# Sums of weight blocks and combinations of h on VectorE in place of POOL, in a two-layer trunk on one core

## Chip, cores and metric

One core of a Trainium2 chip (trn2). The metric is device time in microseconds (us) of one execution of the whole program, the median of the runs. TensorE (PE) multiplies matrices; its weights are loaded by a sequencer that the profile calls PEld. VectorE (DVE), ScalarE (ACT) and GpSimd (POOL) work element by element, SyncE (SP) issues the large transfers. SBUF is the memory on the chip, PSUM the eight banks that TensorE writes to.

## What is computed

Two layers of a hybrid trunk over 512 prompt tokens and 8 sample tokens, all in float32. Each layer is a half-step SwiGLU FFN, a mixing layer (DeltaNet heads beside attention heads), and a second half-step FFN. The change lies in the four FFNs:

```python
def _modulate(x, g, shift, scale):
    return _rms_norm(x, g) * (1.0 + scale) + shift

def _swiglu(h, w_gu, w_down):
    a, b = jnp.split(h @ w_gu, 2, axis=-1)
    return (jax.nn.silu(a) * b) @ w_down

def _layer(x, c, pos, conv_buf, S0, k_buf, v_buf, prm):
...
    m = _adaln(c, w_ada, b_ada)
    h = _modulate(x, g_ffn1, m[:, 0], m[:, 1])
    x = x + 0.5 * m[:, 2] * _swiglu(h, w_ffn1_gu, w_ffn1_down)
...
    h = _modulate(x, g_ffn2, m[:, 6], m[:, 7])
    x = x + 0.5 * m[:, 8] * _swiglu(h, w_ffn2_gu, w_ffn2_down)
    return x, conv_new, S_new, k_new, v_new
```

The model has 1024 features (eight blocks of 128) and 2816 hidden features in each FFN (22 blocks of 128, called f).

## The kernel before

**Layout.** Features lie on the 128 partitions, tokens along the row: 520 columns, in two halves of 256 and 264 (`HALF`, line 23). A float32 product is made of three products in a rounded format: each weight block of 128 x 512 is split into `whi`, a rounded copy that ScalarE makes, and `wlo`, the rest, which VectorE gets as block minus `whi` (`Stream.rest`, line 266); h is split likewise into `hh` and `hl`. TensorE then adds `whi` x `hh`, `whi` x `hl` and `wlo` x `hh`.

**The stream of weights.** `Stream` (line 166) brings weights in: SyncE's queue moves blocks of 128 x 1024 into four raw buffers (two pairs), `advance` (225) issues the transfer of the next block when a raw buffer is free, splits the blocks and puts them into a ring of eight `whi` and `wlo`; `take` (280) hands them to TensorE in order.

**Seven products in place of eight.** For all but the first few f of an FFN, up and gate are computed together by a scheme of Winograd's: `seven` (line 880) makes seven products of 12 matmuls each out of a pair of raw blocks. Its weights are three raw quarters (a11, a12, a22) and four sums of quarters. `add_pair` (189) lists the sums, s1 = a21 + a22, s2 = s1 - a11, s3 = a11 - a21, s4 = a12 - s2; `add_up` (205) issues them when the pair has been sent for. Three f in each FFN (four in the first) are done in the plain way, so there are 75 sevens, and 300 sums. In a seven the products P1 to P7 go to PSUM banks `pb`, `pa`, `pb`, `pc`, `pb`, `pc`, `pb` in turn; `pa` and `pc` are the two banks of one tile that the trace calls `acc`, `pb` is called `aux`. Copies and additions between them (`u1`, `u2`) and the SwiGLU product (`t0`, `t1`: the trace's `g`) follow each product: `g<-acc,u` of 256 columns adds P1 to P2, `g<-acc,u` of 264 adds to P6, `g<-g,aux` multiplies by P7, `g<-g,u` of 264 multiplies the second half, and `ghi`, `glo` split the result for the down projection.

**Combinations of h.** The seven products need three combinations of the blocks of h, made once for each FFN by `combine` (line 798): for each of four k, `y0` and `y1` (each 128 x 2 x 264) out of `ht`, the modulated h before its shift is added, and the shift `sh`; ScalarE and VectorE split these into `th`. The head of an FFN is the stretch in which the norm of x, h, its combinations and the plain f are made, between the last down projection or mixing layer and the first seven.

**Order.** Each engine works through its own queue in order. The code runs once when the program is built; a model of the engines' time (`Clock`, line 40) tells `Stream` how far to run ahead and `Fill` (93) when to put in pieces of side work such as `combine`, which is written as a generator: each `yield` says what must be there before it goes on. All ScalarE work here is issued by `act` (336; its line in the trace is 344), all VectorE work by `_dve` (351; line 352), POOL's by `pool` (361; line 365), matmuls by `mm` (315; line 317), transfers by `dma` (310; line 311).

Of the kernel before, what the change touches and what calls it, by code (L numbers as in the profile page):

```python
# [9 lines left out]
F32 = mybir.dt.float32  # L10
# [155 lines left out]
class Stream:  # L166
# [38 lines left out]
    def add_up(self, j, must):  # L205

        clk = self.ops.clk
        while self.sums and self.sums[0][0] <= j + 2 and self.sums[0][5] < self.nd:
            n, q, x, y, op, d1 = self.sums[0]
            if n > must and clk.ready([self.raw[d1]]) > clk.pe + 1.0:  # L210
                return
            self.sums.pop(0)
            t = self.made[q] = self.new_sum()
            self.ops.pool("tensor_tensor", out=t, in0=self.source(x), in1=self.source(y), op=op)
            self.used(x)
            self.used(y)

# [74 lines left out]
class Ops:  # L292
# [43 lines left out]
    def act(self, **k):  # L336
        func = k["func"]
        if func in TABLE:
            self.table(TABLE[func])
        src = k["in_"]  # L340
        cost = (0.05 if self.psum(src) else 0.093) + 0.000835 * self.cols(src)
        cost += 0.093 * (hasattr(k.get("bias"), "tensor") or hasattr(k.get("scale"), "tensor"))
        cost += 0.093 * ("accum_out" in k)
        self.nc.scalar.activation(**k)  # L344
        self.clk.run("act", cost, self.aps(k, ("out", "accum_out")), self.aps(k, ("in_", "bias", "scale")))
# [15 lines left out]
    def pool(self, f, **k):  # L361
        if f == "memset":
            self.nc.gpsimd.memset(k["out"], k["value"])
        else:
            getattr(self.nc.gpsimd, f)(**k)  # L365
        self.clk.run("pool", 0.1 + 0.003 * self.cols(k["out"]), [k["out"]], self.aps(k, ("in_", "in0", "in1")))

    def tt(self, **k):
        self._dve("tensor_tensor", self.cols(k["out"]), k)

    def stt(self, **k):
        self._dve("scalar_tensor_tensor", self.cols(k["out"]), k)
# [22 lines left out]
def trunk(ctx, tc, xT, cT, cst, rope, vec, gu1, dn1, win, wba, wout, gu2, dn2, ada,  # L395
# [17 lines left out]
    def slot(name, dt=F32, shape=(128, NT), own=False):  # L413
        t = slot_p.tile(list(shape), dt, tag="s", name=name, bufs=SLOTS)
        if not own:
            used.add(t.tensor.name)
        return t

    def drop(*tiles):
        for t in tiles:  # L420
            used.remove(t.tensor.name)
# [376 lines left out]
    def combine(norm, th):  # L798

        ht = norm.ht
        sh = mt[norm.l][:, 3 * norm.j * 8:3 * norm.j * 8 + 8, 0]
        ys = []
        for k in range(4):
            yield lambda: norm.made[1] >= k + 5
            y0, y1 = (slot("y", F32, (128, 2, 264)) for _ in range(2))
            d = slot("d", F32, (128, 264))
            h1, h2 = ht[k], ht[k + 4]
            pool("tensor_tensor", out=y0[:, 0], in0=h1[:, 1], in1=h1[:, 0], op=ALU.subtract)  # L810
            pool("tensor_tensor", out=d, in0=h2[:, 1], in1=h2[:, 0], op=ALU.subtract)
            pool("tensor_tensor", out=y1[:, 1], in0=y0[:, 0], in1=d, op=ALU.subtract)
            drop(d)
            ys.append((y0, y1))
        yield lambda: norm.done[1] >= KD
        ds = small("dsh", (128, 4))
        tt(out=ds, in0=sh[:, 4:8], in1=sh[:, 0:4], op=ALU.subtract)
        xs = []

        def rest(k):  # L820
            (y0, y1), x = ys[k], xs[k]
            tt(out=x[1], in0=y0, in1=x[0].bitcast(F32), op=ALU.subtract)
            tt(out=x[3], in0=y1, in1=x[2].bitcast(F32), op=ALU.subtract)
            drop(y0, y1)
            th.append(x)

        for k in range(4):
            y0, y1 = ys[k]
            yield y0,
            h1, h2 = ht[k], ht[k + 4]  # L830
            stt(out=y0[:, 1], in0=h2[:, 1], scalar=sh[:, k + 4:k + 5], in1=y0[:, 0], op0=ALU.add, op1=ALU.subtract)
            stt(out=y1[:, 0], in0=h2[:, 1], scalar=ds[:, k:k + 1], in1=h1[:, 1], op0=ALU.add, op1=ALU.subtract)
            drop(h1, h2)
            if k:
                rest(k - 1)
            x = [slot("th", F32R, (128, 2, 264)) for _ in range(4)]
            act(out=x[0], in_=y0, func=AF.Copy)
            act(out=x[2], in_=y1, func=AF.Copy)
            xs.append(x)
        yield y1,  # L840
        rest(3)

    def ffn(l, j, norm, nxt, last, first=None, plain=3):
# [36 lines left out]
        def seven():  # L880

            pa, pb, pc = banks.pop(0) if banks else (None, aux(), None)
            if pa is None:
                u = acc()
                pa, pc = u[:, 0], u[:, 1]
            if pb is None:
                pb, pc = aux(), aux()
            t = slot("g")  # L890
            u1, u2 = (slot("u", F32, (128, 2, 264)) for _ in range(2))
            t0, t1 = t[:, 0:256], t[:, 256:520]

            def of_h(a, k0, n):
                return lambda _, part, k: hh[a][part][:, k0 + k, 0:n]

            def of_t(i, c, n=264):
                return lambda _, part, k: th[k][i + part][:, c, 0:n]

            def prod(bank, n, src, first):  # L900
                w = W.take()
                for k in range(4):
                    mmk(bank[:, 0:n], w, k, src, k, 0, first and k == 0, k == 3, join=not first)
                    W.advance(W.out - 1)
                    fill.step()
                go()

            prod(pb, 264, of_h(0, 0, 264), True)
            act(out=u1[:, 0], in_=pb[:, 0:264], func=AF.Copy)
            prod(pa, 256, of_h(0, 4, 256), True)  # L910
            tt(out=t0, in0=pa[:, 0:256], in1=u1[:, 0, 0:256], op=ALU.add)
            prod(pb, 264, of_t(0, 1), False)
            act(out=u1[:, 1], in_=pb[:, 0:264], func=AF.Copy)
            act(out=t0, in_=t0, func=AF.Silu)
            prod(pc, 264, of_t(0, 0), True)
            act(out=u2[:, 1], in_=pc[:, 0:264], func=AF.Copy)
            prod(pb, 264, of_t(2, 0), False)
            act(out=u2[:, 0], in_=pb[:, 0:264], func=AF.Copy)
            prod(pc, 264, of_h(1, 4, 264), False)
            tt(out=t1, in0=pc[:, 0:264], in1=u1[:, 1], op=ALU.add)  # L920
            tt(out=u2[:, 1], in0=u2[:, 1], in1=u2[:, 0], op=ALU.add)
            prod(pb, 256, of_t(2, 1, 256), False)
            act(out=t1, in_=t1, func=AF.Silu)
            tt(out=t0, in0=t0, in1=pb[:, 0:256], op=ALU.mult)

            def end():
                tt(out=t1, in0=t1, in1=u2[:, 1], op=ALU.mult)
                drop(u1, u2)

            later(end, *split(t))  # L930
# [1123 lines left out]
```

## Time and profile before

| | |
|---|---|
| median of 3 runs | 2265.32 us (2263.36 to 2268.89) |
| the profiled execution | 2262.45 us |
| its span, first to last instruction | 2260.2 us |
| mean granted clock of TensorE | 0.980 of full speed |
| TensorE busy (PE), 17254 matmuls | 2146.8 us, 95% |
| weight loads (PEld) | 2018.0 us, 89% |
| VectorE busy | 1590.3 us, 70% |
| ScalarE busy | 1109.7 us, 49% |
| POOL busy | 575.1 us, 25% |

Busy time says how full an engine is, not what sets the end. For that one goes to TensorE's waits, each of which names the engine and the tile that ended it, and from there to the timelines of the other engines at that place: what stood in the queue ahead of the instruction that TensorE waited for, and how long that took. An instruction's duration in a timeline runs from its start to its end; the next one on the same engine can start a little before that end, so the pace of an engine is read from starts.

### The profile page before, as it was taken

Reading aid. Unit: us, or ns where it says so; the run is one execution under the profiler, and the core shown is the slowest. Engines: PE = TensorE matmul, PEld = TensorE weight load, DVE = VectorE, ACT = ScalarE, POOL = GpSimd, SP = SyncE. Lnnn points to the kernel's source line nnn. Section 1 sums busy time; section 2 is a strip of 40 time slices with the busy share of each in tenths; the row PEclk is TensorE's granted clock in tenths of the full one; section 3 lists DMA queues with packets and bytes.
Section 4 is the critical chain, followed back from the end, with each engine's and each line's share of the span. In section 5 each row is a group of like instructions: output and inputs, shape, how many; then the busy total and the mean of one; then the engine's idle time right before and its main releaser. Section 6 shows DMA issues by size and latency. Waiting matters only on the chain. (4 is left out here: it accounts for less than half of the span.)

```text
span 2260.2 us, 44335 instructions
## 1 busy us (share of the span) xinstructions
PE 2146.8 (95%) x17254; PEld 2018.0 (89%) x17254; DVE 1590.3 (70%) x3246; ACT 1109.7 (49%) x2417; POOL 575.1 (25%) x487
## 2 busy tenths in 40 slices
PE   6899999998988999999998999999989889999999
PEld 4798899997877879889998999999888878999999
DVE  5783596567777778448749947955687778865972
ACT  4462365356645446336535634644646445653651
POOL 0440352001021135025305505500010203523530
PEclk9999999999999999999999999999999999999999
DMA  8538634343233564773332332334332242332332
GB/s 283 182 125 306 228 98 140 108 92 97 71 88 91 195 217 152 268 249 113 104 95 66 100 108 89 107 94 107 92 84 79 68 141 72 104 105 92 104 106 72
DMA packets 177538, 287.79 MB, mean 127 GB/s; under 512 B 50448, under 2 KB 96176, under 8 KB 177328
## 3 DMA queue, kind: packets, MB, share of 16 engines
q1 hardware_dynamic: 177328, 284.96, 40.2%
q8 instruction: 135, 2.21, 0.4%
q14 instruction: 75, 0.61, 0.1%
HBM read 271.55 MB, written 14.41 MB: 127 GB/s over the span
## 5 line engine op out<-in xcount | busy, mean ns | idle before, releaser
L344 ACT ACTIVATE whi<-raw 128x512 fp32r<-128x512 f32 (+1 forms) x597 | 361.3, 616 | 397.4 <-PE acc L317 313.2
L352 DVE TENSOR_TENSOR wlo<-raw,whi 128x512 fp32r<-128x512 f32 (+1 forms) x597 | 436.2, 749 | 62.3 <-ACT whi L344 61.3
L317 PE MATMUL acc<-hh,whi 128*128 128x256 f32 (+1 forms) x1640 | 430.9, 299 | 32.3 <-ACT g L344 12.8
L317 PE MATMUL acc<-hh,wlo 128*128 128x256 f32 (+1 forms) x1640 | 409.1, 286 | 12.1 <-DVE wlo L352 12.1
L317 PE MATMUL acc<-hl,whi 128*128 128x256 f32 (+1 forms) x1640 | 408.6, 286 | 1.7 <-DVE hl L352 1.5
L365 POOL TENSOR_TENSOR sum<-raw 128x512 f32<-128x512 f32 x150 | 214.0, 1427 | 662.4 <-DMA raw<-in_gu 384.7
L317 PEld LDWEIGHTS acc<-hh,whi 128*128 128x128 f32 x1640 | 290.8, 192 | 68.8 <-issue 35.8
L352 DVE TENSOR_TENSOR wlo<-sum,whi 128x512 fp32r<-128x512 f32 x300 | 319.4, 1083 | 36.2 <-ACT whi L344 35.2
L317 PE MATMUL aux<-th,whi 128*128 128x264 f32 (+1 forms) x1800 | 335.0, 283 | 1.0 <-ACT u L344 0.9
L317 PEld LDWEIGHTS acc<-hh,wlo 128*128 128x128 f32 x1640 | 289.9, 192 | 14.7 <-DVE wlo L352 14.6
L317 PEld LDWEIGHTS acc<-hl,whi 128*128 128x128 f32 x1640 | 289.6, 192 | 2.6 <-DVE hl L352 2.5
L317 PEld LDWEIGHTS aux<-th,whi 128*128 128x128 f32 x1800 | 277.0, 188 | 4.8 <-issue 3.4
L317 PE MATMUL acc<-ghi,whi 128*128 128x256 f32 (+1 forms) x1320 | 273.9, 283 | 2.7 <-DVE x L352 2.7
L317 PE MATMUL acc<-glo,whi 128*128 128x256 f32 (+1 forms) x1320 | 272.1, 282 | 0.0
L317 PE MATMUL acc<-ghi,wlo 128*128 128x256 f32 (+1 forms) x1320 | 271.6, 282 | 0.0
L317 PE MATMUL aux<-th,wlo 128*128 128x264 f32 (+1 forms) x900 | 254.4, 283 | 0.0
L352 DVE SCALAR_TENSOR_TENSOR x<-acc,mt,x 128x256 f32<-128x256 f32 x136 | 61.6, 480 | 236.0 <-PE acc L317 236.0
L317 PEld LDWEIGHTS acc<-ghi,whi 128*128 128x128 f32 x1320 | 206.4, 188 | 16.8 <-issue 16.8
L344 ACT ACTIVATE whi<-sum 128x512 fp32r<-128x512 f32 x300 | 186.2, 622 | 50.1 <-PE acc L317 45.4
L317 PEld LDWEIGHTS acc<-ghi,wlo 128*128 128x128 f32 x1320 | 207.1, 188 | 0.0
L317 PEld LDWEIGHTS acc<-glo,whi 128*128 128x128 f32 x1320 | 206.8, 188 | 0.0
L317 PE MATMUL aux<-hl,whi 128*128 128x264 f32 x604 | 172.0, 285 | 1.8 <-DVE hl L352 1.7
(325 smaller groups left out, 3979.1 us busy)
## 6 DMA issues: line engine op xcount, KB each, us to landing
raw<-in_gu SPq DMA_DIRECT2D x176, 512.0 KB, 3.6
ada<-in_ada SPq DMA_DIRECT2D x288, 256.0 KB, 5.6
raw<-in_dn SPq DMA_DIRECT2D x64, 512.0 KB, 3.6
raw<-in_win SPq DMA_DIRECT2D x44, 512.0 KB, 3.8
raw<-in_dn SPq DMA_DIRECT2D x64, 192.0 KB, 3.2
raw<-in_wout SPq DMA_DIRECT2D x22, 512.0 KB, 4.5
s<-in_s SPq DMA_DIRECT2D x16, 256.0 KB, 3.8
bv<-vnd SPq DMA_DIRECT2D x16, 256.0 KB, 4.1
```

The lines of the kernel that those rows point to most:

```text
L317: self.nc.tensor.matmul(out, lhsT=lhsT, rhs=rhs, start=start, stop=stop, skip_group_check=join)
L344: self.nc.scalar.activation(**k)
L352: getattr(self.nc.vector, f)(**k)
L365: getattr(self.nc.gpsimd, f)(**k)
```

## The change

Three things are changed. The sums in `add_up` are issued to VectorE. In `combine` the three POOL instructions for each k go; all four parts of `y0` and `y1` are made on VectorE in the loop that follows, three of them with the shift in the same instruction, and there is no tile `d`. In `seven` ScalarE's copy of P5 into `u2[:, 0]` goes; VectorE adds P5 to `u2[:, 1]` from its bank, at once behind P5 and not behind P6.

```diff
--- before.py
+++ after.py
@@ -211,7 +211,7 @@
                 return
             self.sums.pop(0)
             t = self.made[q] = self.new_sum()
-            self.ops.pool("tensor_tensor", out=t, in0=self.source(x), in1=self.source(y), op=op)
+            self.ops.tt(out=t, in0=self.source(x), in1=self.source(y), op=op)
             self.used(x)
             self.used(y)
 
@@ -802,16 +802,6 @@
         ht = norm.ht
         sh = mt[norm.l][:, 3 * norm.j * 8:3 * norm.j * 8 + 8, 0]
         ys = []
-        for k in range(4):
-            yield lambda: norm.made[1] >= k + 5
-            y0, y1 = (slot("y", F32, (128, 2, 264)) for _ in range(2))
-            d = slot("d", F32, (128, 264))
-            h1, h2 = ht[k], ht[k + 4]
-            pool("tensor_tensor", out=y0[:, 0], in0=h1[:, 1], in1=h1[:, 0], op=ALU.subtract)
-            pool("tensor_tensor", out=d, in0=h2[:, 1], in1=h2[:, 0], op=ALU.subtract)
-            pool("tensor_tensor", out=y1[:, 1], in0=y0[:, 0], in1=d, op=ALU.subtract)
-            drop(d)
-            ys.append((y0, y1))
         yield lambda: norm.done[1] >= KD
         ds = small("dsh", (128, 4))
         tt(out=ds, in0=sh[:, 4:8], in1=sh[:, 0:4], op=ALU.subtract)
@@ -825,11 +815,13 @@
             th.append(x)
 
         for k in range(4):
-            y0, y1 = ys[k]
-            yield y0,
+            y0, y1 = (slot("y", F32, (128, 2, 264)) for _ in range(2))
+            ys.append((y0, y1))
             h1, h2 = ht[k], ht[k + 4]
+            tt(out=y0[:, 0], in0=h1[:, 1], in1=h1[:, 0], op=ALU.subtract)
             stt(out=y0[:, 1], in0=h2[:, 1], scalar=sh[:, k + 4:k + 5], in1=y0[:, 0], op0=ALU.add, op1=ALU.subtract)
             stt(out=y1[:, 0], in0=h2[:, 1], scalar=ds[:, k:k + 1], in1=h1[:, 1], op0=ALU.add, op1=ALU.subtract)
+            stt(out=y1[:, 1], in0=h2[:, 0], scalar=sh[:, k + 4:k + 5], in1=y0[:, 1], op0=ALU.add, op1=ALU.subtract)
             drop(h1, h2)
             if k:
                 rest(k - 1)
@@ -837,6 +829,7 @@
             act(out=x[0], in_=y0, func=AF.Copy)
             act(out=x[2], in_=y1, func=AF.Copy)
             xs.append(x)
+            yield ()
         yield y1,
         rest(3)
 
@@ -915,10 +908,9 @@
             prod(pc, 264, of_t(0, 0), True)
             act(out=u2[:, 1], in_=pc[:, 0:264], func=AF.Copy)
             prod(pb, 264, of_t(2, 0), False)
-            act(out=u2[:, 0], in_=pb[:, 0:264], func=AF.Copy)
+            tt(out=u2[:, 1], in0=pb[:, 0:264], in1=u2[:, 1], op=ALU.add)
             prod(pc, 264, of_h(1, 4, 264), False)
             tt(out=t1, in0=pc[:, 0:264], in1=u1[:, 1], op=ALU.add)
-            tt(out=u2[:, 1], in0=u2[:, 1], in1=u2[:, 0], op=ALU.add)
             prod(pb, 256, of_t(2, 1, 256), False)
             act(out=t1, in_=t1, func=AF.Silu)
             tt(out=t0, in0=t0, in1=pb[:, 0:256], op=ALU.mult)
```

VectorE's queue in a seven of the steady part (the last FFN; `wlo<-raw` and `wlo<-sum` are the remainders of raw quarters and of sums, `u` the tile `u2`), from the addition to P6 to the one to P2. Before:

```order
L352 TENSOR_TENSOR g<-acc,u 128x264
L352 TENSOR_TENSOR u<-u 128x264
L352 TENSOR_TENSOR wlo<-sum,whi 128x512
L352 TENSOR_TENSOR g<-g,aux 128x256
L352 TENSOR_TENSOR wlo<-raw,whi 128x512
L352 TENSOR_TENSOR g<-g,u 128x264
L352 TENSOR_TENSOR wlo<-raw,whi 128x512
L352 TENSOR_TENSOR g<-acc,u 128x256
```

and after, from the addition of P5 on:

```order
L352 TENSOR_TENSOR u<-aux,u 128x264
L352 TENSOR_TENSOR wlo<-sum,whi 128x512
L352 TENSOR_TENSOR g<-acc,u 128x264
L352 TENSOR_TENSOR wlo<-sum,whi 128x512
L352 TENSOR_TENSOR sum<-raw 128x512
L352 TENSOR_TENSOR sum<-sum,raw 128x512
L352 TENSOR_TENSOR g<-g,aux 128x256
L352 TENSOR_TENSOR wlo<-raw,whi 128x512
L352 TENSOR_TENSOR g<-g,u 128x264
L352 TENSOR_TENSOR wlo<-raw,whi 128x512
L352 TENSOR_TENSOR sum<-raw 128x512
L352 TENSOR_TENSOR g<-acc,u 128x256
```

Three sums now stand between the addition to P6 and the one to P2, two ahead of the multiplication by P7 and one behind it; the fourth comes behind the row that ends the second piece.

VectorE's queue at the head of layer 1's first FFN (`hl` with its number is the remainder of h, `dsh` the differences of the shift, `y` the combinations). Before:

```order
L352 TENSOR_TENSOR wlo<-raw,whi 128x512 x3
L352 TENSOR_TENSOR g<-g,acc 128x256
L352 SCALAR_TENSOR_TENSOR hl_77<-ht,mt_81,hh_76 128x256 x2
L352 TENSOR_TENSOR dsh<-mt_81 128x4
L352 SCALAR_TENSOR_TENSOR y<-ht,mt_81,y 128x264
L352 SCALAR_TENSOR_TENSOR y<-ht,dsh 128x264
L352 TENSOR_TENSOR g<-g,aux 128x264 x2
```

and after:

```order
L352 TENSOR_TENSOR wlo<-raw,whi 128x512 x3
L352 TENSOR_TENSOR sum<-raw 128x512
L352 TENSOR_TENSOR sum<-sum,raw 128x512
L352 TENSOR_TENSOR g<-g,acc 128x256
L352 SCALAR_TENSOR_TENSOR hl_77<-ht,mt_81,hh_76 128x256 x2
L352 TENSOR_TENSOR dsh<-mt_81 128x4
L352 TENSOR_TENSOR y<-ht 128x264
L352 SCALAR_TENSOR_TENSOR y<-ht,mt_81,y 128x264
L352 SCALAR_TENSOR_TENSOR y<-ht,dsh 128x264
L352 SCALAR_TENSOR_TENSOR y<-ht,mt_81,y 128x264
L352 TENSOR_TENSOR y<-ht 128x264
```

Two sums come in ahead of `hl`, and each k has four rows for `y` where two were.

ScalarE's queue at the same head. Before:

```order
L344 ACTIVATE whi<-raw 128x512 x4
L344 ACTIVATE hh_76<-ht,mt_81 128x256
L344 ACTIVATE th<-y 128x528 x2
L344 ACTIVATE g<-aux 128x264 x2
L344 ACTIVATE whi<-raw 128x512 x2
```

and after:

```order
L344 ACTIVATE whi<-raw 128x512 x4
L344 ACTIVATE hh_76<-ht,mt_81 128x256
L344 ACTIVATE th<-y 128x528 x4
L344 ACTIVATE g<-aux 128x264 x2
L344 ACTIVATE whi<-raw 128x512 x2
```

The copies of two k stand ahead of the `g` that empties the banks, where those of one k stood.

## Rows read from the trace of the kernel before

**Rows 1.** Page, part 1: busy us (share of the span) and instructions of each engine.

```profile
PE 2146.8 (95%) x17254; PEld 2018.0 (89%) x17254; DVE 1590.3 (70%) x3246; ACT 1109.7 (49%) x2417; POOL 575.1 (25%) x487
```

**Rows 2.** TensorE's waits: engine, line, what it waited for: total us, times, longest us.

```profile
PEld acc L317 <- DVE wlo L352: 15.4, 13, 3.7
PEld acc L317 <- DVE g L352: 14.8, 45, 1.1
...
PEld acc L317 <- ACT g L344: 13.2, 2, 7.5
...
PEld acc L317 <- ACT whi L344: 9.5, 4, 3.1
```

**Rows 3.** Timeline of VectorE, a seven: start, us, line, operation, count, [idle before <- releaser].

```profile
2120.58 0.41 DVE L352 TENSOR_TENSOR g<-g,aux 128x256 f32<-128x256 f32 x1
2120.92 1.46 DVE L352 TENSOR_TENSOR wlo<-raw,whi 128x512 fp32r<-128x512 f32 x1
...
2122.64 0.68 DVE L352 TENSOR_TENSOR wlo<-raw,whi 128x512 fp32r<-128x512 f32 x1
2123.25 0.41 DVE L352 TENSOR_TENSOR g<-acc,u 128x256 f32<-128x256 f32 x1
...
2128.36 0.43 DVE L352 TENSOR_TENSOR g<-acc,u 128x264 f32<-128x264 f32 x1 [0.45 <-PE acc L317]
...
2130.99 0.41 DVE L352 TENSOR_TENSOR g<-g,aux 128x256 f32<-128x256 f32 x1
```

**Rows 4.** Timeline of PEld, the same seven.

```profile
2123.71 0.30 PEld L317 LDWEIGHTS acc<-th,whi 128*128 128x128 f32 x2 [0.35 <-DVE g L352]
```

**Rows 5.** Timeline of ScalarE, the same seven.

```profile
2120.73 0.39 ACT L344 ACTIVATE u<-aux 128x264 f32<-128x264 f32 x1 [0.90 <-PE aux L317]
```

**Rows 6.** Page, part 5: groups xcount | busy us, mean ns | idle before, releaser.

```profile
L365 POOL TENSOR_TENSOR sum<-raw 128x512 f32<-128x512 f32 x150 | 214.0, 1427 | 662.4 <-DMA raw<-in_gu 384.7
...
L352 DVE TENSOR_TENSOR wlo<-sum,whi 128x512 fp32r<-128x512 f32 x300 | 319.4, 1083 | 36.2 <-ACT whi L344 35.2
```

**Rows 7.** Timeline of POOL and of SyncE's queue, the same seven.

```profile
2126.05 1.32 POOL L365 TENSOR_TENSOR sum<-raw 128x512 f32<-128x512 f32 x1 [4.22 <-DMA raw<-in_gu]
...
2122.40 2.24 SPq L311 DMA_DIRECT2D raw<-in_gu  x2
```

**Rows 8.** Timeline of VectorE, head of layer 1's first FFN.

```profile
1202.28 0.97 DVE L352 SCALAR_TENSOR_TENSOR ht<-x,mt,rs 128x256 f32<-128x256 f32 x1
...
1203.51 3.24 DVE L352 TENSOR_TENSOR wlo<-raw,whi 128x512 fp32r<-128x512 f32 x3
...
1208.44 0.71 DVE L352 TENSOR_TENSOR dsh<-mt 128x4 f32<-128x4 f32 x1
1209.08 1.59 DVE L352 SCALAR_TENSOR_TENSOR y<-ht,mt,y 128x264 f32<-128x264 f32 x1
...
1226.43 0.48 DVE L352 SCALAR_TENSOR_TENSOR y<-ht,mt,y 128x264 f32<-128x264 f32 x1
1226.84 0.48 DVE L352 SCALAR_TENSOR_TENSOR y<-ht,dsh 128x264 f32<-128x264 f32 x1
```

**Rows 9.** Timeline of ScalarE and PEld at three heads.

```profile
1226.95 1.18 ACT L344 ACTIVATE th<-y 128x528 fp32r<-128x528 f32 x2 [3.25 <-DVE y L352]
...
1229.24 0.29 PEld L317 LDWEIGHTS acc<-hh,whi 128*128 128x128 f32 x1 [5.73 <-ACT g L344]
...
806.00 0.50 PEld L317 LDWEIGHTS acc<-hh,whi 128*128 128x128 f32 x2 [2.89 <-ACT whi L344]
...
1919.84 0.30 PEld L317 LDWEIGHTS acc<-hh,whi 128*128 128x128 f32 x2 [1.85 <-ACT whi L344]
```

**Rows 10.** Windows: us, busy us by engine, PEclk, DMA share, GB/s.

```profile
75.50:85.70 10.20, 5.75 (x26) 5.75 (x27) 9.50 (x14) 3.90 (x8) 3.86 (x4) 0.50 0.73 255
806.00:809.40 3.40, 3.23 (x14) 1.76 (x18) 3.40 (x7) 3.40 (x8) 0.00 (x0) 0.51 0.34 80
1225.80:1232.60 6.80, 2.93 (x12) 2.63 (x12) 6.10 (x13) 3.75 (x8) 0.00 (x0) 0.50 0.00 0
```

## The prediction

> **What bounds the kernel now.** I read the totals first: TensorE works 2146.8 us of the 2260.2 us span, VectorE 1590.3, ScalarE 1109.7, GpSimd (POOL) 575.1 [rows 1]. So the time can fall only where TensorE waits, and moving work off POOL is worth nothing by itself. Next the list of TensorE's waits, by the sequencer that loads weights (PEld) and what released it [rows 2]. Three lines there are of the kind this change touches: 14.8 us in 45 waits for VectorE's `g`, 13.2 us in two waits for ScalarE's `g`, 9.5 us in four for `whi`. A fourth, 15.4 us for `wlo`, is touched at its edge. The first line belongs to the pairs of up and gate blocks that `seven` computes, the other two to the heads of the four FFNs. I took one of each apart.
>
> *One seven.* VectorE's rows from 2120.58 to 2130.99 are one period, from one `g<-g,aux` to the next: 10.41 us [rows 3]. TensorE waits in it once, 0.35 us, for VectorE's `g` [rows 4]. Without that wait the period is 10.06 us, 1.44 for each of the seven products. What TensorE waits for is `g<-acc,u` of 256 columns, which adds the second product to the first: the fourth product is written to the other bank of the same tile and starts when that read is over. It starts at 2123.25, and by ScalarE's copy of the first product [rows 5] this is 2.52 us after the first product ended. It is late because the `wlo` at 2120.92 took 1.46 us, where the one at 2122.64, with the same shape, took 0.68 [rows 3]. The difference is POOL. Over the kernel, `wlo<-sum` takes a mean of 1083 ns, and a POOL sum of two raw blocks 1427 ns [rows 6]; VectorE's slow rows lie where POOL's sums run.
>
> **The change, part by part.** The profiled execution took 2262.45 us, 2.87 under the median of the three runs (2265.32); I subtract from the former and add 2.87 at the end.
>
> *The 300 sums.* They leave POOL and are now VectorE's, four to a seven. VectorE alone starts the next instruction 0.61 us after one of 512 columns (2122.64 to 2123.25) and 0.34 us after one of 256 (2120.58 to 2120.92) [rows 3]. A seven has on VectorE, after the change, 11 instructions of 512 columns (seven `wlo`, four sums), `glo` of 520, and five of 256 or 264: 11 x 0.60 + 0.61 + 5 x 0.345 = 8.94 us in 10.06 us of TensorE. VectorE fits, at 89%. But it works in order, so I laid the new order of one seven out in time, from the end of the first product (0) to that of the next (10.06), at these paces and with POOL quiet. VectorE runs empty once before the end of the sixth product, as it does now (0.45 us idle for `acc` at 2128.36 [rows 3]), and that sets the clock: sixth product 7.19, `g<-acc,u` of 264 until 7.53, a `wlo` until 8.13, first sum until 8.73, second sum, which needs the first one, until 9.41, `g<-g,aux` until 9.75, `wlo`, `g<-g,u`, `wlo` until 11.29, third sum until 11.89, and there the `g<-acc,u` of 256 starts. That is 1.83 us after the next first product's end, against 2.52 now: 0.69 us earlier, where 0.35 us of wait are to be had. The wait goes, with 0.34 us to spare. What is late next is the addition in `u`: it now waits for the end of the fifth product (15.81), is done at 16.15 and is wanted when the seventh overwrites the bank, near 16.9: 0.7 us to spare. So the 14.8 us of [rows 2] go: **-14.8**. Bounds: 0 if the cover of 0.34 fails, and at the other end half of the 15.4 us for `wlo` [rows 2] as well, another 7.7, since those waits are placed behind slowed rows too.
>
> *The first sum and its transfer.* POOL's first sum starts when the raw blocks land: 4.22 us idle for the transfer, at 2126.05, 3.65 us after SyncE issued it at 2122.40 [rows 7]. On VectorE that wait would stand in front of everything. In the new order the first sum starts at 8.13, and the `wlo` whose end releases the raw buffers, the one behind `g<-g,aux`, ends near 0.4 (10.4 in the seven before), so the transfer has 7.7 us where the row shows 3.65. I take nothing for it; it comes back among the rivals.
>
> *Up's second half from its bank.* 75 copies of 264 columns leave ScalarE (0.39 us each by a row of that kind [rows 5]) and VectorE's addition reads the bank. ScalarE is busy for half of the span [rows 1]: 0, with the 0.7 us above as cover; if the cover is gone, 0.1 us late costs 7.5 us over 75 sevens.
>
> *The combinations of h.* Three POOL instructions and two of VectorE for each of four k become four of VectorE, ready one behind the other. Before, `y` was made by POOL while VectorE scaled h, both slowed: an `ht` row takes 0.97 us at 1202.28 and the first `y` 1.59 us at 1209.08, where two `y` with POOL quiet start 0.41 us apart (1226.43, 1226.84) [rows 8]. ScalarE's copies `th<-y` wait for that, 3.25 us at 1226.95, and the `g` that empties TensorE's bank stands behind them in ScalarE's queue: TensorE waits 5.73 us [rows 9]. I queued this head (layer 1, first FFN) anew. The last `hl` ends at 1208.44 now [rows 8]. Six `ht` and `hl` at 0.41 for some 0.9 give 2.9 back, three `wlo` 1.4 (3.24 for the three [rows 8], against 1.83), two sums cost 1.2: 1205.3. From there to the last `y`: 16 instructions for `y`, 4 x (0.34 + 3 x 0.41) = 6.3, at most six for `th` at 0.62 (an estimate from 0.61 at 512 columns) 3.7, two `g` 0.7, six `wlo` 3.7, two sums 1.2: 15.6, so 1220.9. ScalarE's two copies, a `whi` and the way between the engines then take it to about 1222.9. TensorE now begins its wait at 1229.24 - 5.73 = 1223.5. All 5.73 go, with 0.6 to spare. Behind the wait TensorE's granted clock is 0.50 of full speed, 1.2 GHz for 2.4, up to 1232.6 [rows 10]; 3.4 us at half speed from 1229.24 on cost 1.7. Sum **-7.4** (bounds 0 and -8.5 with the small waits before it).
>
> The other three heads I did not queue to the end. Layer 0's second FFN waits 2.89 us for `whi` at 806.00 [rows 9], and the clock is at 0.51 for 3.4 us behind it [rows 10], another 1.7: **-4.6** (0 to -4.6). Layer 1's second waits 1.85 us [rows 9]: **-1.85** (0 to -1.85). Layer 0's first FFN has the 7.5 us wait of [rows 2], and half speed up to 85.70 [rows 10], 5.75 us of it with TensorE at work, which is 2.9. There VectorE's sums stand behind transfers that fill 0.73 of the engines' time [rows 10], so I take about half of the wait: **-4.0** (0 to -10.4). The heads make -17.85.
>
> Total: -14.8 - 17.85 = -32.65, so 2229.8 profiled and **2232.5 us** for the median. With the far bounds of the gains (6.4 more at layer 0's first head, 7.7 for `wlo`) it would be 2218; with half of the seven's gain and a third of the heads' lost, 2246.
>
> **The rivals.**
> *The sevens keep waiting (2247.4, chance 0.13).* The cover of 0.34 us rests on 15 durations taken from a quiet VectorE. If each 512-column instruction costs 0.05 more, or a sum is put where one too many stands ahead of `g<-acc,u`, the wait stays and only the heads gain: 2265.3 - 17.9. For it: nine tenths of VectorE's time are taken. Against it: rows 2122.64 to 2123.25.
>
> *VectorE pays each row's whole duration (2250, chance 0.04).* If the next instruction started only at the end of the one before, the seven would need 11 x 0.68 + 0.69 + 5 x 0.42 = 10.27 us of VectorE, more than the 10.06 of TensorE, and VectorE would set the pace. 75 x 10.27 is 1.0 us more than 75 x 10.06 + 14.8, so nothing is left of the sevens' gain, and the heads, longer by some 2, give 16: 2250. This speaks against the change. The rows speak against it: starts are 0.61 apart where the durations are 0.68 [rows 3]. The Trainium skill says it of VectorE ("VectorE: DVE Perf Modes", section "The DRAIN you can't avoid"): the next operation does not start until the pipe of the one before is empty. The trace agrees only in part, 0.61 us being less than the 0.68 that an instruction is shown to last.
>
> *The heads don't gain (2250.5, chance 0.09).* The waits at the heads are put off to another link, the four `th` copies that now stand ahead of `g` in ScalarE's queue instead of two, or the sums in front of `y`: 2265.3 - 14.8.
>
> *New waits eat both (2265, chance 0.07).* VectorE, the only engine left for it, delays `wlo` here and there by what is gained elsewhere; or VectorE's rows stay as long on the chip without POOL's sums as with them.
>
> *Slower: VectorE stands still for a transfer (2285, chance 0.07).* Place: the first sum of each pair, at 8.13 in the seven, with `g<-g,aux`, two `wlo` and `g<-acc,u` behind it. Point: a transfer of 7.7 us. Each us beyond is lost in each seven. Half a us beyond it in 75 sevens is 37.5, the heads still give 17.9, and 14.8 is not gained: 2265.3 + 37.5 - 17.9 = 2285. For it: POOL's sums have 384.7 us of idle time that a transfer ended [rows 6], and VectorE has none to give. Against it: 3.65 us in the steady part.
>
> **How the numbers follow.** Forecast 0.60, the rivals 0.13, 0.04, 0.09, 0.07 and 0.07. A measurement of this kernel tells 0.3% from no change, so faster means under 2258.5 and slower over 2272: faster is 0.60 + 0.13 + 0.04 + 0.09 = 0.86, same 0.07, slower 0.07. The range goes from 2217, just under the far bound of the gains, to 2252, which takes in the three rivals that gain one half; what is left out is the last two rivals and the edges, under 0.2.
>
> **What would show it.** `wlo<-sum` at a mean near 0.68 us where it was 1083 ns; the wait for VectorE's `g` gone from TensorE's list, and a period of 10.06 us; no wait of 5.73 or 2.89 us at the heads and a granted clock of 1.0 behind them; VectorE near 75% of the span. It would be wrong if VectorE's first sum shows idle time for the transfer, if `g<-acc,u` starts more than 2.2 us after the first product's end, or if TensorE waits for `wlo` for more than the 15.4 us of now.

## The result

The changed kernel takes 2232.88 us (median of 4 runs, 2228.65 to 2234.35), the one before 2265.71 (4 runs, 2263.36 to 2268.89): a ratio of 0.9851, 95% interval 0.9833 to 0.9869, or 33 us less. The forecast was 2232.5. That the medians agree within 0.4 us is in part luck. The two profiled executions, from which all rows come, took 2262.45 and 2234.35, which is 28.1 us apart, where the sum said 32.65; and the experiments show that the sum credited one term to one edit where another edit removes the same wait by itself, and that another term gave 4.5 us where the sum had 7.4.

The page's first part after [rows 1]:

```profile
PE 2135.6 (96%) x17254; PEld 2014.9 (90%) x17254; DVE 1554.2 (70%) x3578; ACT 1091.2 (49%) x2342; POOL 79.7 (4%) x139
```

TensorE's work is as it was, 17254 matmuls; POOL's fell from 575.1 to 79.7 us. VectorE did 332 more instructions and was busy 36 us less: what it no longer lost beside POOL is more than what it took over. TensorE's waits after, in the columns of [rows 2]:

```profile
PEld acc L317 <- DVE wlo L352: 13.6, 12, 3.2
...
PEld acc L317 <- ACT g L344: 5.4, 2, 4.0
...
PEld acc L317 <- ACT whi L344: 4.8, 2, 3.1
...
PEld acc L317 <- DVE g L352: 3.7, 6, 1.5
...
PEld aux L317 <- ACT u L344: 2.9, 2, 2.6
```

VectorE's `g` fell from 14.8 us in 45 waits to 3.7 in 6, ScalarE's `g` from 13.2 to 5.4, `whi` from 9.5 to 4.8, `wlo` from 15.4 to 13.6. Of the lines in the FFNs one grew, ScalarE's `u`, from 1.5 us to 2.9.

A **steady seven** after. VectorE, then ScalarE, in the columns of [rows 3]:

```profile
2104.60 0.41 DVE L352 TENSOR_TENSOR g<-g,aux 128x256 f32<-128x256 f32 x1
...
2106.48 0.69 DVE L352 TENSOR_TENSOR sum<-raw 128x512 f32<-128x512 f32 x1
2107.08 0.42 DVE L352 TENSOR_TENSOR g<-acc,u 128x256 f32<-128x256 f32 x1
...
2111.09 0.43 DVE L352 TENSOR_TENSOR u<-aux,u 128x264 f32<-128x264 f32 x1 [0.58 <-PE aux L317]
...
2112.47 0.43 DVE L352 TENSOR_TENSOR g<-acc,u 128x264 f32<-128x264 f32 x1 [0.34 <-PE acc L317]
...
2114.74 0.41 DVE L352 TENSOR_TENSOR g<-g,aux 128x256 f32<-128x256 f32 x1
```

```profile
2105.20 0.39 ACT L344 ACTIVATE u<-aux 128x264 f32<-128x264 f32 x1 [0.89 <-PE aux L317]
```

The period from `g<-g,aux` to `g<-g,aux` is 10.14 us (2104.60 to 2114.74), where [rows 3] have 10.41. `g<-acc,u` of 256 columns starts 1.88 us after ScalarE's copy of the first product (2107.08 - 2105.20); the prediction laid it at 1.83, and it was 2.52. VectorE now runs empty twice in a seven, 0.58 us before the fifth product ends and 0.34 before the sixth. The part of eleven sevens of the last FFN, in windows from its first matmul with `th` to its last (columns of [rows 10]), before and after:

```profile
2080.85:2192.37 111.52, 110.37 (x901) 108.60 (x900) 98.17 (x138) 70.52 (x150) 54.62 (x36) 1.00 0.34 103
```

```profile
2055.68:2164.30 108.62, 108.62 (x901) 108.62 (x900) 94.64 (x176) 67.68 (x139) 0.00 (x0) 1.00 0.34 104
```

Before, TensorE works 110.37 of 111.52 us; after, all of 108.62. The part is 2.9 us shorter, and TensorE has no wait left in it. (1.15 of the 2.9 us stood as idle time in the row before, the rest within TensorE's recorded work there.)

The **groups** on VectorE (columns of [rows 6]):

```profile
L352 DVE TENSOR_TENSOR wlo<-sum,whi 128x512 fp32r<-128x512 f32 x300 | 199.2, 683 | 9.2 <-ACT whi L344 7.3 <-PE acc L317 2.0
L352 DVE TENSOR_TENSOR sum<-raw 128x512 f32<-128x512 f32 x150 | 102.7, 685 | 4.7 <-DMA raw<-in_gu 4.7
```

`wlo<-sum` went from a mean of 1083 ns to 683, as forecast, and a sum takes 685 where POOL took 1427. All sums together waited 4.7 us for transfers; POOL had 384.7 us of such idle time [rows 6].

From the times of the same matmul in both traces, before minus after, the gain stage by stage in us (TensorE's matmuls for the modulation of the next layers were put in other places in layer 0; they are moved back here at about 0.12 us each, which leaves some 0.2 us open in layer 0's rows):

```
                              forecast   measured
head, layer 0 first FFN          4.0        5.7
  its 7 sevens, 11 sevens                  -1.3, +2.9
head, layer 0 second FFN         4.6        3.9
  its 8 sevens, 11 sevens                  +0.4, +3.1
head, layer 1 first FFN          7.4        4.5
  its 8 sevens, 11 sevens                  -1.9, +3.0
head, layer 1 second FFN         1.85       3.6
  its 8 sevens, 11 sevens                  +1.2, +2.9
all heads                       17.85      17.7
all sevens                      14.8       10.3
the two mixing layers            0         -1.7, +2.2
the rest                         0         -1.0
```

(The measured column sums to 27.5, the difference of the spans to 27.6.)

### The profile page after: what moved, and what is told of

Read it like the earlier page. It is cut to its first block, busy times and chain, and to the rows that moved or that the text cites. A ratio compares the mean times of both kernels' runs of the same rounds, so it can differ in the third digit from the quotient of the medians.

```text
span 2232.6 us, 43833 instructions
## 1 busy us (share of the span) xinstructions
PE 2135.6 (96%) x17254; PEld 2014.9 (90%) x17254; DVE 1554.2 (70%) x3578; ACT 1091.2 (49%) x2342; POOL 79.7 (4%) x139
## 3 DMA queue, kind: packets, MB, share of 16 engines
q8 instruction: 135, 2.21, 0.4%
## 4 chain that ended last, share of the span: by engine, by line
PE 81%; DVE 10%; issue 5%; ACT 2%; DMA 1%; POOL 0%; SPq 0%; DVEq 0%; POOLq 0%; ACTq 0%
PE acc L317 46%; PE aux L317 34%; DVE wlo L352 2%; DVE s L352 1%; PE aux L327 1%; ACT sq L344 1%; DVE t L352 1%; DVE hl L352 1%; DVE w L352 1%; ACT whi L344 0%; DVE y L352 0%; DVE x L352 0%; DVE cy L352 0%; DVE sum L352 0%; DMA ada<-in_ada 0%
## 5 line engine op out<-in xcount | busy, mean ns | idle before, releaser
L352 DVE TENSOR_TENSOR wlo<-raw,whi 128x512 fp32r<-128x512 f32 (+1 forms) x597 | 390.6, 672 | 58.6 <-ACT whi L344 57.7
L317 PEld LDWEIGHTS acc<-hh,wlo 128*128 128x128 f32 x1640 | 288.9, 191 | 13.6 <-DVE wlo L352 13.6
L352 DVE TENSOR_TENSOR wlo<-sum,whi 128x512 fp32r<-128x512 f32 x300 | 199.2, 683 | 9.2 <-ACT whi L344 7.3
L317 PE MATMUL aux<-hh,whi 128*128 128x264 f32 x604 | 172.9, 286 | 0.0
```

Source lines behind the costliest of these rows:

```text
L317: self.nc.tensor.matmul(out, lhsT=lhsT, rhs=rhs, start=start, stop=stop, skip_group_check=join)
L352: getattr(self.nc.vector, f)(**k)
```

## The experiments

The question that the result leaves: which of the three edits did it, and by what. Theory 1 is the prediction's: POOL's sums slow VectorE, so `g<-acc,u` is late in the seven, and moving the sums frees it. Its rivals are told with each run. The medians of the kernel before that were measured beside these runs lie between 2264.9 and 2265.7. The last column is the part of eleven sevens of the last FFN, cut from the windows as above.

```
                                   median    ratio, 95% interval        eleven sevens
before                             2265.7                                  111.52
sums alone on VectorE              2243.5    0.9901 [0.9888, 0.9915]       109.34
combinations alone                 2256.0    0.9953 [0.9941, 0.9966]       111.99
addition from the bank alone       2254.9    0.9951 [0.9938, 0.9965]       108.55
all but the sums                   2248.3    0.9930 [0.9915, 0.9946]       108.71
all but the combinations           2236.9    0.9871 [0.9855, 0.9888]       108.65
all but the bank                   2237.5    0.9876 [0.9859, 0.9892]       109.60
all three                          2232.9    0.9851 [0.9833, 0.9869]       108.62
```

### One edit at a time

The kernel before with the sums alone moved:

```diff
-            self.ops.pool("tensor_tensor", out=t, in0=self.source(x), in1=self.source(y), op=op)
+            self.ops.tt(out=t, in0=self.source(x), in1=self.source(y), op=op)
```

> The kernel before with one part of the change alone: the 300 sums on VectorE; the combinations of h and up's copy stay as before. Theory 1 (VectorE's rows are slow because POOL reads SBUF at the same time): the wait for g<-acc,u goes from the steady sevens, 0.27 us for each, and the heads keep most of their waits, since POOL still makes y: 2265.5 - 11 - 4 = 2250 (2246 to 2255), and the trace has a full part of 11 sevens near 108.4 us where before has 111.4. Theory 2 (the wait goes because the addition of P5 and the copies stand elsewhere, not because of POOL's sums): 2262 to 2266, and a full part stays at 111.4.

Measured 2243.5, below what either theory gave. The full part fell to 109.34, as theory 1 said, but 0.7 us of its wait remain; and the heads and mixing layers gained about 9 us where I had allowed 4.

The combinations alone (`combine` of the change in the kernel before):

> The kernel before with one part alone: the combinations of h on VectorE; the sums stay on POOL. Theory 1: the sevens keep their 0.27 us each, the heads lose the waits that came from POOL's work on y, but POOL's sums still slow VectorE there: 2265.5 - 10 = 2255 (2250 to 2260). Theory 2 for the heads (they gain because the sums left, not the combinations): 2264 to 2267.

Measured 2256.0: as theory 1 said. The full part stays as it was (111.99).

The addition from the bank alone:

```diff
             prod(pb, 264, of_t(2, 0), False)
-            act(out=u2[:, 0], in_=pb[:, 0:264], func=AF.Copy)
+            tt(out=u2[:, 1], in0=pb[:, 0:264], in1=u2[:, 1], op=ALU.add)
             prod(pc, 264, of_h(1, 4, 264), False)
             tt(out=t1, in0=pc[:, 0:264], in1=u1[:, 1], op=ALU.add)
-            tt(out=u2[:, 1], in0=u2[:, 1], in1=u2[:, 0], op=ALU.add)
```

> The kernel before with one part alone: P5 added from its bank, 75 copies fewer on ScalarE. Theory 1: no change, 2265.5 (2263 to 2268), g<-acc,u is as late as before. Theory 2 (this edit is what makes g<-acc,u early, one slow addition fewer ahead of it): 2253 to 2258, and a full part of 11 sevens under 110 us.

Measured 2254.9, and the full part 108.55: theory 1 falls here as the whole account. POOL makes all its sums in this kernel, and yet TensorE has one wait for `g` left in this part, of 0.22 us (columns of [rows 10]):

```profile
2078.05:2186.60 108.55, 108.54 (x902) 108.27 (x900) 96.09 (x138) 68.61 (x139) 58.11 (x36) 1.00 0.33 104
```

VectorE and ScalarE in one of its sevens:

```profile
2116.92 1.46 DVE L352 TENSOR_TENSOR wlo<-raw,whi 128x512 fp32r<-128x512 f32 x1
...
2119.25 0.41 DVE L352 TENSOR_TENSOR g<-acc,u 128x256 f32<-128x256 f32 x1
...
2123.13 0.43 DVE L352 TENSOR_TENSOR u<-aux,u 128x264 f32<-128x264 f32 x1 [1.02 <-PE aux L317]
```

```profile
2117.29 0.39 ACT L344 ACTIVATE u<-aux 128x264 f32<-128x264 f32 x1 [0.90 <-PE aux L317]
```

The `wlo` behind `g<-g,aux` is as slow as before (1.46 us, [rows 3] have 1.46), but it starts earlier in the seven: `g<-acc,u` begins 1.96 us after the first product's copy (2119.25 - 2117.29), not 2.52. This is one seven of many: in the nine between the first and the last of this part the distance goes from 1.74 to 2.38 us, in the kernel before from 2.32 to 3.13, as POOL's sums fall on other rows each time. The reason is in the addition itself. In the seven of [rows 3] it stands between the sixth product and `g<-g,aux`:

```profile
2128.71 0.65 DVE L352 TENSOR_TENSOR u<-u 128x264 f32<-128x264 f32 x1
2129.28 1.78 DVE L352 TENSOR_TENSOR wlo<-sum,whi 128x512 fp32r<-128x512 f32 x1
```

From start to start it holds the queue for 0.57 us (2129.28 - 2128.71), which is the 0.56 by which `g<-acc,u` is earlier here. Its group in the kernel before, and in this one:

```profile
L352 DVE TENSOR_TENSOR u<-u 128x264 f32<-128x264 f32 x75 | 49.4, 659 | 0.0
```

```profile
L352 DVE TENSOR_TENSOR u<-aux,u 128x264 f32<-128x264 f32 x75 | 32.3, 430 | 51.3 <-PE aux L317 50.9 <-issue 0.3
```

With both inputs in SBUF the addition took 659 ns on average: 739 in the 56 rows that overlap a sum of POOL by 0.1 us or more, 422 in the other 19. With one input in PSUM it takes 430, though POOL is as busy and `wlo<-sum` still takes 986 on average; 53 of its 75 rows overlap a sum, and none of them takes over 435. And it has moved from the crowded stretch behind the sixth product into idle time behind the fifth (1.02 us idle ahead of it at 2123.13). No run has the one without the other. So theory 3: the wait of the fourth product has a point, near 2.1 us behind the first product, and each of two edits alone brings `g<-acc,u` past that point or within 0.1 us of it.

### Two edits at a time

The changed kernel without the sums' move:

> The changed kernel with the sums back on POOL (combinations on VectorE and the addition from the bank stay). Theory 3, formed after the bank edit alone freed the steady sevens: either edit is enough there, since each brings g<-acc,u forward past the point at which the fourth product would start; then the steady part stays at 108.5 us and the loss against the changed kernel comes from the heads and first sevens alone: 2264.9 - 8.9 - 10.0 = 2246 (2242 to 2250). Theory 1 (what frees the sevens is that POOL is quiet): 2254 to 2258, a full part back at 111.4.

Measured 2248.3 (six runs, one of them at 2257.0), by theory 3; the full part is 108.71 with POOL at work for half of it:

```profile
2069.47:2178.18 108.71, 108.71 (x901) 108.65 (x900) 94.06 (x138) 68.50 (x139) 57.33 (x36) 1.00 0.33 104
```

So of the 15.4 us that the sums are worth beside the other two edits, the four parts of eleven sevens hold none: they differ from the changed kernel's by 0.3 us at most. What the sums bring there is all in the heads, the sevens right behind them and the mixing layers; whether by POOL's reads that end there or by sums that come earlier, no run takes apart.

Without the bank edit:

> The changed kernel with up's second half as before (ScalarE copies P5, VectorE adds it behind P6); sums and combinations on VectorE. Theory 3 (sums and bank edit both free the same wait, the sums alone leave 0.09 us in each seven): the bank edit is worth 75 x 0.09 = 7 here, so 2233 + 7 = 2240 (2237 to 2243). If the three parts add up as they did alone: 2264.9 - 21.4 - 8.9 = 2234.6.

Measured 2237.5, between the two, 4.6 us above the changed kernel. The full parts are each 1.0 to 1.3 us longer, 4.5 in all, as theory 3 says; what the expectation added for the short parts, the heads even out. In the last part `g<-acc,u` starts 2.21 to 2.22 us behind the first product's copy, where the changed kernel has 1.88: with POOL quiet, the old addition's place costs 0.33 us of the queue.

Without the combinations:

> The changed kernel with the combinations of h as before (three of five instructions for each k on POOL); sums on VectorE and the addition from the bank stay. By the sevens alone (the sums' run less the 0.09 us that it leaves in each seven): 2243.5 - 7 = 2236.5, so the combinations are worth 3 to 4 here. If they keep the 8.9 that they gave alone: 2233 + 9 = 2242.

Measured 2236.9, by the account of the sevens. The three edits gave 21.4, 8.9 and 10.0 us alone (counted from the median of 2264.9 beside them), 40.3 together; taken out of the whole one at a time they cost 15.4, 4.0 and 4.6, that is 24.0. The whole is 32.8. They overlap because they pull at the same queue.

### The place in the queue: one more instruction ahead of `g<-acc,u`

An addition of two constant tiles that nothing needs is put on VectorE, in the changed kernel (256 columns, and in the second kernel 512):

```diff
+            nc.vector.tensor_tensor(out=W.dc[:, 0:256], in0=cs[:, 0:256], in1=cs[:, 512:768], op=ALU.add)
             tt(out=t0, in0=pa[:, 0:256], in1=u1[:, 0, 0:256], op=ALU.add)
```

> The changed kernel with one instruction more on VectorE in each seven, an addition of two constant tiles of 256 columns that nothing needs, right ahead of g<-acc,u (0.34 us from start to start). It uses up the cover of 0.34 us that the prediction gave this place. g<-acc,u then starts 1.88 + 0.34 = 2.22 us behind the first product. By the prediction's cover: 2233 to 2236. By the run with the sums alone, whose g<-acc,u starts 2.21 behind and whose period is 0.09 longer: 75 x 0.09 = 7, 2240.

> The same with 512 columns (0.60 us). g<-acc,u starts 1.88 + 0.60 = 2.48 us behind the first product, about where the kernel before has it (2.52, with a wait of 0.35): 75 x 0.30 = 22, so 2255 (2248 to 2260). If VectorE's total is what counts (9.5 us of 10.1 a seven, still under TensorE's), not the place in its queue: 2233.

Measured 2239.7 (ratio to the kernel before 0.9889, 0.9876 to 0.9902) and 2256.65 (0.9960, 0.9947 to 0.9973): 7 and 24 us lost. VectorE with 256 columns, and ScalarE's copy of the first product:

```profile
2108.73 0.41 DVE L352 TENSOR_TENSOR g<-g,aux 128x256 f32<-128x256 f32 x1
...
2111.55 0.42 DVE L352 TENSOR_TENSOR g<-acc,u 128x256 f32<-128x256 f32 x1
...
2118.96 0.41 DVE L352 TENSOR_TENSOR g<-g,aux 128x256 f32<-128x256 f32 x1
```

```profile
2109.34 0.39 ACT L344 ACTIVATE u<-aux 128x264 f32<-128x264 f32 x1 [0.91 <-PE aux L317]
```

VectorE with 512 columns, ScalarE's copy of the first product, and the weight load that waits:

```profile
2137.38 0.68 DVE L352 TENSOR_TENSOR sum<-raw 128x512 f32<-128x512 f32 x1
2137.99 0.68 DVE L905 TENSOR_TENSOR dc<-cs 128x512 f32<-128x512 f32 x1
2138.59 0.42 DVE L352 TENSOR_TENSOR g<-acc,u 128x256 f32<-128x256 f32 x1
```

```profile
2136.11 0.39 ACT L344 ACTIVATE u<-aux 128x264 f32<-128x264 f32 x1 [0.90 <-PE aux L317]
```

```profile
2139.06 0.30 PEld L317 LDWEIGHTS acc<-th,whi 128*128 128x128 f32 x2 [0.30 <-DVE g L352]
```

`g<-acc,u` starts 2.48 us after the copy at 2136.11 (the sum of 1.88 and 0.60), the fourth product waits 0.30 and the period is 10.51, though VectorE is busy for only 101.08 us of the 111.93 of the full part and still runs empty ahead of the fifth and sixth products. It is the place in the queue that costs, not the sum of work. With 256 columns it starts 2.21 us behind (2111.55 - 2109.34) and the period is 10.23 (2118.96 - 2108.73), 0.09 more than in the changed kernel: so the point lies near 2.12 (with 512, 2.48 less 0.37 gives 2.11), and the cover of the changed kernel is 0.24 us, not 0.34.

### What slows VectorE: POOL's reads

The changed kernel, with POOL given two constant tiles to add behind each sum; its output `dc` is used by nothing:

```diff
             self.ops.tt(out=t, in0=self.source(x), in1=self.source(y), op=op)
+            pl.tensor_tensor(out=dc[:, 0:8], in0=t[:, 0:8], in1=cs[:, 0:8], op=ALU.mult)
+            pl.tensor_tensor(out=dc, in0=cs[:, 0:512], in1=cs[:, 512:1024], op=ALU.add)
```

> The changed kernel with work added that nothing needs: behind each of the 300 sums on VectorE, POOL reads eight columns of it (to keep its pace) and then adds two constant tiles of 128 x 512. VectorE's own instructions and their order are those of the changed kernel. Theory 1: VectorE's rows beside it get slow again; in the kernel before four POOL sums cost a seven about 2.5 us of VectorE (1.6 on wlo<-sum, the rest on others), so VectorE needs 8.9 + 2.5 = 11.4 us where TensorE needs 10.1, and each seven loses 1.3: 2233 + 98 = 2331 (2290 to 2400), slower than the kernel before too. Theory 2: POOL's work beside VectorE costs nothing, the sums were only late: 2231 to 2236.

In the second kernel the last line is three fills of `dc` (`pl.memset(dc, 0.0)`).

> The changed kernel with work added that nothing needs: behind each sum POOL reads eight columns of it, as in the run with reads, but then fills a tile of 128 x 512 three times in place of adding two tiles: about 1.6 us of POOL (525 ns for one fill in the kernel before) that reads no SBUF. Theory A (POOL's reads are what slows VectorE): 2233 (2231 to 2240). Theory B (any work of POOL on SBUF does): near the 2421 of the run with reads.

Measured 2421.3 (ratio 1.0685, 1.0670 to 1.0700) with the additions, 2230.4 (0.9850, 0.9836 to 0.9863) with the fills. With the fills POOL was busier than it had ever been, and VectorE's rows did not notice:

```profile
L218 POOL MEMSET dc<- 128x512 f32 x900 | 473.8, 526 | 52.2
```

```profile
L356 DVE TENSOR_TENSOR wlo<-sum,whi 128x512 fp32r<-128x512 f32 x300 | 198.9, 682 | 9.3 <-ACT whi L348 7.3 <-PE acc L321 2.0
```

With the additions, VectorE and POOL in one seven:

```profile
2300.17 1.78 DVE L355 TENSOR_TENSOR wlo<-raw,whi 128x512 fp32r<-128x512 f32 x1
...
2302.48 0.41 DVE L355 TENSOR_TENSOR g<-acc,u 128x256 f32<-128x256 f32 x1
...
2304.02 1.79 DVE L355 TENSOR_TENSOR glo<-g,ghi 128x520 fp32r<-128x520 f32 x1
```

```profile
2300.03 1.36 POOL L217 TENSOR_TENSOR dc<-cs 128x512 f32<-128x512 f32 x1
...
2303.63 1.62 POOL L217 TENSOR_TENSOR dc<-cs 128x512 f32<-128x512 f32 x1
```

`wlo` beside POOL's addition takes 1.78 us for 0.68 and `glo` 1.79 for 0.69; the rows that meet none of POOL's additions, as `g<-acc,u` at 2302.48, take what they take alone. The direction was theory 1's; the price was not. I took 2.5 us for each seven from the means of the kernel before, and expected 1.3 of loss; this seven lasts 13.4 (`g<-acc,u` at 2302.48 and at 2315.89), 3.3 more, and the mean loss is 188 / 75 = 2.5. Each of POOL's additions holds up a row of VectorE by about 1.1 us, four make 4.4, and VectorE has 10.06 - 8.94 = 1.1 us to spare, where without the four sums it had 3.5. The Trainium skill tells this in "SBUF — State Buffer", section "Who interferes with whom": a VectorE instruction with two inputs in SBUF contends with a POOL instruction that reads SBUF, and not with one that only writes it. The three runs agree, with 2421.3, 2230.4 and the 430 ns of the addition from a bank in the kernel with that edit alone.

### Each sum one product later

```diff
-        while self.sums and self.sums[0][0] <= j + 2 and self.sums[0][5] < self.nd:
+        while self.sums and self.sums[0][0] <= j + 1 and self.sums[0][5] < self.nd:
```

> The changed kernel with each sum issued one product later (two products ahead becomes one). In a seven, two sums stand ahead of g<-acc,u in place of three; at the head of layer 1's first FFN two sums leave the stretch ahead of hl, where VectorE is the bound. If the head's remaining waits come from VectorE's queue there, they shrink by up to the 1.3 us of two sums, with half a granted clock behind them up to 3: 2230 (2228 to 2233). If only the steady sevens mattered: 2233, no change. Against it: with one product less of lead a whi or wlo of a sum can come late, 0.3 us in each seven would be 22, 2255.

Measured 2232.7 (0.9852, 0.9837 to 0.9866): no change. At the head of layer 1's first FFN the waits moved and did not shrink:

```profile
1208.73 0.19 PEld L317 LDWEIGHTS acc<-hh,whi 128*128 128x128 f32 x1 [1.92 <-ACT g L344]
...
1211.64 0.30 PEld L317 LDWEIGHTS aux<-th,whi 128*128 128x128 f32 x2 [1.44 <-ACT u L344]
...
1215.77 0.30 PEld L317 LDWEIGHTS acc<-th,whi 128*128 128x128 f32 x2 [2.61 <-DVE g L352]
```

1.92, 1.44 and 2.61 us, 6.0 in all, where the changed kernel has 1.33, 2.60 and 0.92, 4.9 (below). Work taken from ahead of one link of the head stood ahead of the next.

## Why the prediction was right, and where it was not

**The seven's timing: right.** `g<-acc,u` at 1.88 us for 1.83, a period of 10.14 for 10.06, sums and `wlo` 0.60 us from start to start, the addition in `u` behind the fifth product. VectorE is as full as the sum said (94.64 us of the full part's 108.62, 87%, for 89%; over the span it stayed at 70%, where I had written 75), and the rival in which it pays each row's whole duration is out: in the kernel with 512 columns more, the two rows of 0.68 us and the one behind them start 0.61 and 0.60 apart. The section of the Trainium skill cited for that rival ("VectorE: DVE Perf Modes", section "The DRAIN you can't avoid") has an exception that the prediction left out: a next operation that is not held starts earlier. These rows do start earlier, by 0.07 to 0.08 us.

**The sevens' term: too large, and credited to one edit alone.** The prediction gave -14.8 to the 300 sums and 0 to the bank ("0, with the 0.7 us above as cover"). The waits for VectorE's `g` fell by 11.1; the four parts of eleven sevens gained 11.9 us, the sevens right behind the heads lost 1.6, and the 10.3 that are left are 4.5 short of the term, about what the whole sum is off (28.1 for 32.65). And the bank edit alone frees the steady sevens, at 108.55 us a part, while the sums alone leave 0.7 to 1.2 us in each. The step that failed is the costing of the bank edit by ScalarE's saving and by the place where the result is wanted. I did not ask what the old addition cost VectorE, which stood in [rows 3]'s queue between the sixth product and `g<-g,aux`, slowed like the others. Laying out the queue with that edit alone, POOL still at work, would have shown it.

**The cover: 0.24 for 0.34.** The two kernels with one instruction more put it there. 0.34 us more ahead of `g<-acc,u` cost 7 us and 0.60 cost 24, more than the 14.8 that the rival of the failing cover allowed. (On the way from the sixth product to `g<-acc,u` that the prediction laid out stand nine rows; it speaks of 15 durations. And its last sum, 2229.8 and 2.87, makes 2232.7, where it wrote 2232.5.)

**The heads: their total right by luck, 17.7 for 17.85, their parts not.** Two heads gave some 1.7 us more than their terms each, and two 0.7 and 2.9 less. The largest term, -7.4 for layer 1's first FFN, came out at 4.5, of which the sevens behind it give 1.9 back. VectorE, ScalarE and the weight loads there, in the columns of [rows 8] and [rows 9]:

```profile
1190.17 1.90 DVE L352 TENSOR_TENSOR wlo<-raw,whi 128x512 fp32r<-128x512 f32 x3 [2.58 <-ACT whi L344]
...
1194.43 0.16 DVE L352 TENSOR_TENSOR dsh<-mt 128x4 f32<-128x4 f32 x1
...
1209.08 0.49 DVE L352 SCALAR_TENSOR_TENSOR y<-ht,mt,y 128x264 f32<-128x264 f32 x1
...
1211.32 0.68 DVE L352 TENSOR_TENSOR sum<-raw 128x512 f32<-128x512 f32 x1
1212.04 0.70 DVE L352 TENSOR_TENSOR sum<-sum,raw 128x512 f32<-128x512 f32 x1
1212.65 0.76 DVE L352 TENSOR_TENSOR g<-g,acc 128x256 f32<-128x256 f32 x2
```

```profile
1213.44 0.64 ACT L344 ACTIVATE ghi<-g 128x520 fp32r<-128x520 f32 x1 [2.12 <-DVE g L352]
...
1215.03 0.37 ACT L344 ACTIVATE u<-aux 128x264 f32<-128x264 f32 x1
```

```profile
1211.37 0.19 PEld L317 LDWEIGHTS acc<-hh,whi 128*128 128x128 f32 x1 [1.33 <-ACT g L344]
...
1215.45 0.30 PEld L317 LDWEIGHTS aux<-th,whi 128*128 128x128 f32 x2 [2.60 <-ACT u L344]
...
1218.85 0.50 PEld L317 LDWEIGHTS acc<-th,whi 128*128 128x128 f32 x2 [0.92 <-DVE g L352]
```

From the last `hl` (before 1194.43) to the last `y` (1209.57) it takes 15.1 us; the queue said 15.6. What failed is the step ahead of it, "1205.3", the 3.1 us by which `hl` was to end earlier. The changed kernel is 13.1 us ahead when this head begins, so 1194.43 stands for 1207.5 of before: 0.9 earlier than 1208.44. I had subtracted shorter durations from a stretch in which VectorE has idle time: at 1190.17 it waits 2.58 us for `whi`. So `g` comes late and TensorE waits 1.33 us in place of 5.73. Then the wait goes on in another form, the case that I had named as a rival for the heads (0.09): ScalarE's copy `u` at 1215.03 stands behind a `ghi` that waits 2.12 us for VectorE's `g<-g,acc` (1212.65), and that stands behind two sums. TensorE waits 2.60 us for it, and 0.92 for the first `g<-acc,u`.

The clock's term, -1.7, failed too. TensorE's granted clock is still at half speed behind these waits, now in the first sevens (columns of [rows 10]):

```profile
1215.30:1222.20 6.90, 6.13 (x27) 5.83 (x28) 6.51 (x12) 3.30 (x9) 0.00 (x0) 0.53 0.39 110
```

6.13 us of work at a clock of 0.53 cost near 3 us (an estimate, half of the work), more than the 3.4 us at half speed did before. In layer 0's first head the prediction's half of the wait was about right: 4.02 of 7.5 us are left; of the rest of the 5.7, 1.3 us are gained ahead of that wait and 0.9 behind it, where the clock is at half speed for 3.4 us and was for 10.2. In layer 1's second head the wait of 1.85 us is gone as forecast; a clock at half speed for 3.4 us, where it was for 6.8, gives about 1.1 more.

**What was in no term: the mixing layers,** -1.7 and +2.2 us. TensorE's order of matmuls is the same there. In layer 0 one us of the loss lies between the same matmuls, before and after:

```profile
704.50:714.50 10.00, 7.42 (x47) 7.15 (x48) 9.89 (x36) 7.25 (x24) 0.00 (x0) 0.83 0.57 171
```

```profile
696.50:706.50 10.00, 8.12 (x44) 7.84 (x45) 9.00 (x32) 6.38 (x19) 0.00 (x0) 0.66 0.59 170
```

The granted clock is 0.66 where it was 0.83. Another 1.6 us are lost right behind, at a clock of 0.81 (706.50 to 715.50) where it was 1.00 (714.50 to 722.50). Why the clock fell at one time and not at the other I have not tested.

**The slower rival** did not come about: VectorE's sums waited 4.7 us for transfers in all, and in a seven `sum<-raw` follows the row before it at once.

## What to carry to other kernels

When several edits touch one in-order queue, lay the queue out for each edit alone as well as for all: here two of three each removed the same wait, or all but 0.1 us of it, and one that was costed at nothing on the engine it relieved did its work on another. What decides is how late the one instruction starts that TensorE waits for, and its distance from the point at which it begins to cost can be measured with an instruction that does nothing, in front of it. Before shortening a chain at the start of a stage, see whether its engine had idle time there: what is taken off ahead of a wait for another engine is not gained.

## What was not expected of the hardware

An addition on VectorE with one input in PSUM keeps its pace beside POOL (430 ns in the kernel with POOL's sums, 433 in the changed one), where the same addition from SBUF took 659 beside them and 424 in the kernel with the sums alone moved, whose POOL is quiet. POOL's fills cost VectorE nothing, 474 us of them; 440 us of POOL's additions cost 188 us. And a POOL instruction of eight columns took 481 ns on average in the run with additions and 658 in the run with fills, where another of that size (`ht`) takes 261 in the kernel before; what held it up there I have not taken apart.
